# Layer border of a two-layer decoder trunk: three features made by VectorE, two more weight blocks held ahead, and the memory branch's outputs split together

## The chip, the cores and the metric

The kernel runs on one core of a Trainium2 chip. The time is the device time in microseconds of one execution; lower is better. The core has five engines that run side by side: TensorE (PE in the profile) multiplies matrices, VectorE (DVE) and ScalarE (ACT) work on tiles element by element, GpSimd (POOL) does little here, and SyncE (SP) issues the transfers from and to memory. Each engine takes its own instructions strictly in the order in which they were written, and waits on semaphores for the others.

## The reference

Two layers, each with four branches that all read the same x (512 tokens, 1024 features):

```
h = x @ w_in[l]                       # columns are shared out among the branches
y_rwkv = RWKV-7 recurrence(h...)      y_mla  = causal latent attention(h...)
y_conv = 31-tap convolution(h...)     y_mem  = attention into 256 memory tokens:
    kv = mem @ w_mem_kv;  s = q k / sqrt(128);  softmax(s) v
each branch:  y * silu(its gate columns of h)
proj   = y_n @ w_o_branch[l, n]       # per branch
merged = sum_n sigmoid(merge columns of h + b_gate) * proj
out    = merged @ w_out[l]
x      = LayerNorm(alpha * x + out) * ln_g + ln_b
```

The result of the second layer is the output.

## The kernel before

**Arithmetic.** Features lie on the partitions and tokens along the free dimension, so a projection makes 128 features by 512 tokens in PSUM. To keep fp32 accuracy with fast matmuls, every operand is split into a high half (a cast, on ScalarE as a rule) and a low half (the operand less its high half, on VectorE): `split`, line 503. Each product is then three matmuls (`mm3`, line 580). Tiles that end in h and l are such halves.

**Weights.** They are streamed. A block of 128 x 1024 numbers is loaded into one of two raw tiles (`WR = 2`, line 32), split into a high and a low tile of a pool with three pairs (`WH = 3`), and used; w123 is the 124th block, w123h and w123l its halves. `prefetch` in `stream` (line 2234) asks for the next block when fewer than `LOOK = 4` blocks are held ahead and a raw tile is free. The transfers go out on SyncE's queue (line 371).

**Order.** The kernel is written as generators: a stream of matmul items, and tasks for everything that hangs on them. At build time a planner (`Plan`, line 70) keeps a clock for each engine and a cost for each operation, and writes the instructions in the order in which its clocks let them go. So a small change of one task can move many others. Nearly all instructions go through one helper, so the profile shows line 265 for VectorE, ScalarE and GpSimd, 359 for matmuls and 364 for transposes on TensorE; groups are told apart by tile names.

**The layer border.** The second half of the output projection is the item z1 (`second_item`, line 2001; tiles pz, block 117 to 120). Its sums go through the layer norm (`out_after` and `norm`: z, lbs, lmv, lrs, lnb) and are stored to memory as xtok. To cover this, the planned `ORDER` (line 26) puts the next layer's memory work around it: keys m0 and m1 ahead of z1, keys m2 and m3 behind it (tile ps_mk, blocks 121 and 122), then m4, the memory values (`values` in `memory_items`, line 704; tile pmv, blocks 123 to 126, twelve matmuls each). Between those, `features` (line 2149) turns the normalised z back into features: four transposes into a PSUM tile xT, then xf (scale by ln_g and add ln_b), its high half xh and its low half xl; eight features, with two PSUM tiles to share. After that layer 1 begins with the latent projections (tile pl, blocks 127 on).

**The memory branch.** Four heads of attention into memory (tiles xs, xP, xt, xo) are interleaved with latent attention (scores ms, weights mP, transposes mt, output mo) and with projections and convolution taps (cacc on VectorE). Each head ends in a tile xy, which is multiplied by its gate and then split (`gate_items`, line 1830; halves yxg0 to yxg3) for the merge, which reads them much later. `turn(n)` (line 1827) says when a branch may split its outputs; for the memory branch (n = 3) it always says yes. `scaled` (line 649) gives a softmax's scaling to ScalarE or VectorE, whichever has the earlier clock in the planner.

Of the kernel before, what the change touches and what calls it, by code (L numbers as in the profile page):

```python
# [15 lines left out]
AF = mybir.ActivationFunctionType  # L16
ALU = mybir.AluOpType
# [11 lines left out]
PRI = {}  # L29
GATHER = 1500.0  # L30
RIDE = 4000.0
WR = 2
WH = 3
ALPHA = (2.0 * LAYERS) ** 0.25
# [35 lines left out]
class Plan:  # L70
# [96 lines left out]
    def run(self, stream):  # L167
# [4 lines left out]
        while True:  # L172
# [10 lines left out]
            wait = last + GATHER if self.cut == (128, 128) and not over else 0.0  # L183
            ride = RIDE if self.cut == (128, 128) and not over and last else 0.0

# [153 lines left out]
def trunk_kernel(ctx: ExitStack, tc: tile.TileContext, A, out, dbg=None):  # L339
    nc = tc.nc  # L340
    plan = Plan(tc.keep_in_program_order)
    V, S, G = Engine(plan, nc.vector, "DVE"), Engine(plan, nc.scalar, "ACT"), Engine(plan, nc.gpsimd, "POOL")
# [30 lines left out]
    def pool(bufs, **k):  # L373
        return Space(plan, ctx.enter_context(tc.tile_pool(bufs=bufs, **k)), bufs)
# [24 lines left out]
    def u(name, cols=512, dt=F32, p=128):  # L399
        return up.tile([p, cols], dt, tag="u", name=name)  # L400
# [105 lines left out]
        yield  # L506
        V.tensor_tensor(out=dst_l, in0=src, in1=dst_h.bitcast(F32), op=ALU.subtract)

    wlive = {"raw": 0, "n": 0, "hl": {}}

    x0 = []

    def weights(name, src, parts, last=False):
# [4 lines left out]
        cols = sum(parts)  # L518
        raw = wp.tile([128, 1024], F32, tag="wr", name=name, bufs=WR)[:, 0:cols]
        first = name == "w0"  # L520
# [148 lines left out]
    def close_phase():  # L669
        phase[0].close()  # L670

    def memory_items(l):

        ms = []
        res = {}

        def load(pool):
            raws = []
            for i in range(4):
                raws.append(u(f"mr{i}_{l}"))  # L680
                DMA(raws[i], A["memT"][:, 512 * i:512 * i + 512])
            hl = [[pool(f"mem{n}{i}_{l}") for n in "hl"] for i in range(4)]
            for x in "kv":
                res[x] = [[u(f"{x}m{n}{i}_{l}", 512, F32R) for n in "hl"] for i in range(2)]
            for i, (h, lo) in enumerate(hl):
                plan.due(raws[i])
                yield
                yield from split(h, lo, raws[i])
                for b in range(2):
                    c = slice(256 * b, 256 * b + 256)  # L690
                    ms.append((h[:, c], lo[:, c]))

        def keep(x, i, c, ps):
            h, lo = (y[:, c] for y in res[x][i])
            return split(h, lo, ps)

        def keys(h):
            def run(get):
                ps = yield from project(get, ms, f"mk{h}_{l}", 256)
                yield from keep("k", h // 2, slice(256 * (h % 2), 256 * (h % 2) + 256), ps)  # L700
                yield
            return run

        def values(get):
            if l:
                ps = yield from pg.take([128, 512], f"pmv{l}", 2)
            else:
                ps = [pp.tile([128, 512], F32, tag="pp", name=f"pmv0_{l}")]
                ps += yield from pa.take([128, 512], f"pmv1_{l}")
            yield from wide(get, ps, lambda k, b: [x[:, 128 * b:128 * b + 128] for x in ms[k]])  # L710

            def after():
                for i in range(2):
                    yield from keep("v", i, slice(0, 512), ps[i])
                    if l:
                        pg.free()
                if l == 0:
                    pa.free()
                MEM[l] = (res["k"], res["v"])
            plan.spawn(after())  # L720
            yield

        its = [([(A["w_mk"][l, h], (512, 512))], keys(h)) for h in range(4)]
        its += [([(A["w_mv"][l, i], (512, 512)) for i in range(4)], values)]
        return load, its, lambda: len(ms) == 8

    def layer_items(l):
        items = []
# [3 lines left out]
        def pr(n, i=0, w=1):  # L732
            return PRM[l][0][:, PCOL[n] + i:PCOL[n] + i + w]
# [749 lines left out]
        ymem = [None] * 4  # L1483
# [341 lines left out]
        added = [0] * 4  # L1825

        def turn(n):
            return n == 3 or added[{1: 3, 2: 1, 0: 2}[n]] >= 8

        def gate_items(n, base, name, ready, ys, res, op):  # L1830
            for i in range(4):
# [92 lines left out]
        def end_items():  # L1924
# [76 lines left out]
            def second_item():  # L2001

                def run(get):
                    wb = []
                    for tbs in ((0, 1), (2,), (3,)):
                        ps = yield from pg.take([128, 512], f"pz1{tbs[0]}" + t_, len(tbs))
                        for k in range(8):
                            if len(wb) <= k:
                                wb.append((yield from get()))
                            h, lo = wb[k]  # L2010
                            for o, tb in zip(ps, tbs):
                                mm3(o, *(x[:, 128 * tb:128 * tb + 128] for x in merged[k]), h, lo, k == 0, k == 7)
                            if tbs[-1] == 3:
                                free(h)
                            if k in (1, 3, 5):
                                yield

                        def after(tbs=tbs, ps=ps):
                            for o, tb in zip(ps, tbs):
                                yield from out_after(tb, o, 512)  # L2020
                                pg.free()
                        plan.spawn(after())
                        yield

                item("z1", [(A["w_out"][l, 1, i], (512, 512), i > 0 and (lambda: gates[0] == 8)) for i in range(4)], run)
# [123 lines left out]
            def features(k, zs):  # L2149
                ps, = yield from pa.take([128, 512], f"xT{k}" + t_)  # L2150
                plan.due(*zs)
                yield
                for tb in range(4):
                    TR(ps[:, 128 * tb:128 * tb + 128], zs[tb])
                yield
                f = u(f"xf{k}" + t_)
                h = xp.tile([128, 512], F32R, tag="xh", name=f"xh{k}_{l + 1}")
                lo = xp.tile([128, 512], F32R, tag="xl", name=f"xl{k}_{l + 1}")
                S.activation(f, ps, AF.Identity, scale=pr("ln_g", k), bias=pr("ln_b", k))
                pa.free()  # L2160
                turned[0] += 1
                yield from split(h, lo, f)
                while len(X[l + 1]) < k:
                    yield lambda: len(X[l + 1]) == k
                X[l + 1].append((h, lo))
                if k == 7:
                    close_phase()
                    closed[l] = True
# [46 lines left out]
    def stream(items):  # L2215


        items, todo, held, runs = list(items), [], [], []
        count, look = [0], [3]

        def pick():
            for n, (blocks, run, ready, _, _) in enumerate(items):
                if not blocks and ready is None:
                    if n == 0:
                        return n
                    break
                if ready is None or ready():
                    return n
            for n, (blocks, run, ready, _, soon) in enumerate(items):
                if soon and soon():  # L2230
                    return n
            return None

        def prefetch():
            while len(held) < look[0] + (0 if items else 2) and wlive["raw"] < WR:
                if not todo:
                    n = pick()
                    if n is None:
                        return
                    blocks, run, _, picked, _ = items.pop(n)  # L2240
                    if picked:
                        picked()
                    todo.extend(blocks)
                    runs.append(run)
                    if not blocks:
                        continue
                held.extend(weights(f"w{count[0]}", *todo.pop(0)))
                count[0] += 1

        def get():  # L2250
            while not held:
                prefetch()
                if not held:
                    yield lambda: wlive["raw"] < WR
            if not held[0]:
                yield lambda: held[0]
            w = held.pop(0)
            prefetch()
            yield plan.when(*w)
            return w  # L2260

        while items or runs:
            prefetch()
            if not runs:
                yield lambda: wlive["raw"] < WR and pick() is not None
                continue
            for cond in runs[0](get):
                prefetch()
                yield cond
            runs.pop(0)  # L2270
            look[0] = LOOK
# [106 lines left out]
```

## Time and profile before

| what | value |
|---|---|
| median of 3 runs | 1456.66 us (1456.55 to 1457.02) |
| the profiled execution, device time | 1457.49 us |
| its span, first to last instruction | 1455.5 us |
| TensorE busy | 1442.5 us (99%) |
| TensorE weight loads | 1213.7 us (83%) |
| VectorE busy | 1094.3 us (75%) |
| ScalarE busy | 690.8 us (47%) |
| TensorE's granted clock, mean | 0.999 |
| chain that ended last, share on TensorE | 94% |

The page gives one profiled execution. The timeline shows instructions with start, duration, operation and names (written tile, arrow, read tiles), and in brackets how long the engine sat idle before it and what it waited for. Matmuls overlap: the end of a matmul is modelled and lies behind the start of the next, so the distance between starts tells how fast TensorE really goes.

### The profile page before, as it was taken

How to read it: one execution, taken by the hardware profiler on the slowest of the kernel's cores; microseconds unless marked ns; L12 is line 12 of the kernel's file. 1: busy time of each engine (PE TensorE's matmuls, PEld its weight loads, DVE VectorE, ACT ScalarE, POOL GpSimd, SP SyncE). 2: the span in 40 equal slices, each digit the busy share in tenths (PEclk: the TensorE clock that was granted, in tenths of full speed). 3: DMA queues.
4: the chain of work that ended last, by engine and by line, in shares of the span. 5: the costliest groups of instructions: out<-in, count | busy, mean ns of one | idle time of the engine just before them, and what ended most of it. 6: DMA issues, size and time to landing. Idle time of an engine off the chain costs nothing.

```text
span 1455.5 us, 28372 instructions
## 1 busy us (share of the span) xinstructions
PE 1442.5 (99%) x11481; PEld 1213.7 (83%) x11481; DVE 1094.3 (75%) x2245; ACT 690.8 (47%) x1325; POOL 45.1 (3%) x79
## 2 busy tenths in 40 slices
PE   9999999999999999999999999999999999999997
PEld 9888888888888888888889878888888888888886
DVE  6799988878767786544654889988888796856756
ACT  5557754354542533443254566553263635334331
POOL 0000000000000000000000000000000000000003
PEclk9999999999999999999999999999999999999999
DMA  7454342333323233434344251622423332324422
GB/s 222 126 141 105 96 122 84 96 99 87 101 74 101 81 89 93 147 100 133 113 156 122 62 145 55 167 73 73 122 74 96 93 103 79 102 80 150 154 90 85
DMA packets 94279, 156.16 MB, mean 107 GB/s; under 512 B 44354, under 2 KB 52290, under 8 KB 94148
## 3 DMA queue, kind: packets, MB, share of 16 engines
q1 hardware_dynamic: 94148, 154.35, 36.5%
q8 instruction: 90, 1.47, 0.4%
q14 instruction: 41, 0.34, 0.1%
HBM read 135.37 MB, written 6.10 MB: 97 GB/s over the span
## 4 chain that ended last, share of the span: by engine, by line
PE 94%; DVE 3%; ACT 1%; DMA 1%; issue 0%; SPq 0%; DVEq 0%; ACTq 0%
PE ps_m L359 24%; PE po L359 12%; PE pz L359 3%; PE ps_cg L359 3%; PE ps_r L359 3%; PE ps_mg L359 3%; PE ps_val L359 3%; PE ps_rg L359 3%; PE ps_k L359 3%; PE ps_v L359 3%; PE ps_xg L359 3%; PE ps_glu L359 2%; PE ps_xq L359 2%; PE pl L359 2%; PE ms L359 2%; PE ps_mk L359 2%
## 5 line engine op out<-in xcount | busy, mean ns | idle before, releaser
L265 DVE SCALAR_TENSOR_TENSOR cacc<-hpad,prm,cacc 128x512 f32<-128x512 f32 x240 | 178.6, 746 | 3.3
L265 ACT ACTIVATE tm<-ps_m,prm 128x512 f32<-128x512 f32 x64 | 44.4, 693 | 169.4 <-PE ps_m L359 169.3
L265 DVE SCALAR_TENSOR_TENSOR mt<-tm,po 128x512 f32<-128x512 f32 x48 | 32.9, 685 | 69.3 <-PE po L359 69.1
L265 ACT ACTIVATE mP<-ms,nmm 128x128 f32<-128x128 f32 (+3 forms) x64 | 33.5, 527 | 10.1 <-DVE nmm L265 4.7
L265 DVE TENSOR_TENSOR merged<-merged,mt 128x512 f32<-128x512 f32 x48 | 33.2, 692 | 1.7
L265 DVE CUSTOM_DVE_ANT_0 ms<-ms,causal 128x128 f32<-128x128 f32 (+3 forms) x64 | 30.6, 499 | 0.3 <-PE ms L359 0.2
L265 ACT COPY mPT<-mt 128x256 f32<-128x256 f32 (+3 forms) x64 | 25.8, 429 | 8.2 <-PE mt L364 8.0
L364 PE MATMUL mt<-cst,mP 128*128 128x128 f32 x160 | 26.3, 275 | 1.6 <-DVE mP L265 1.4
L364 PEld LDWEIGHTS mt<-cst,mP 128*128 128x128 f32 x160 | 19.7, 140 | 8.9 <-DVE mP L265 1.6
L265 ACT ACTIVATE yb<-yb,mr,gr 128x64 f32<-128x64 f32 x64 | 22.1, 430 | 3.1 <-DVE mr L265 3.1
L265 DVE TENSOR_TENSOR pr<-ax,bc 128x256 f32<-128x256 f32 x64 | 22.7, 415 | 0.0
L265 POOL MEMSET D<- 128x8 f32 x8 | 0.9, 114 | 697.8 <-PE ms L359 267.6
L265 DVE SCALAR_TENSOR_TENSOR merged<-tm,po 128x512 f32<-128x512 f32 x16 | 11.0, 685 | 14.7 <-PE po L359 14.5
L265 ACT ACTIVATE Zd<-zq,cst 64x128 f32<-64x128 f32 (+1 forms) x48 | 19.2, 400 | 4.9 <-DMA zq<-scrr 4.3
L359 PE MATMUL ms<-kTl,qT 96*128 96x128 f32 (+3 forms) x64 | 21.4, 334 | 0.0
L359 PE MATMUL ms<-kTh,qTl 96*128 96x128 f32 (+3 forms) x64 | 20.6, 322 | 0.0
L359 PE MATMUL ms<-kTh,qT 96*128 96x128 f32 (+3 forms) x64 | 20.6, 321 | 0.0
L265 DVE TENSOR_REDUCE ax<-pr 128x32 f32<-128x512 f32 x32 | 20.3, 674 | 0.0
L359 PEld LDWEIGHTS mo<-mPT,v 128*64 128x64 f32 x320 | 17.3, 137 | 2.6 <-issue 2.1
L359 PE MATMUL mo<-mPT,v 128*64 128x128 f32 x320 | 19.2, 275 | 0.0
L265 ACT ACTIVATE z<-z,lnb,lrs 128x256 f32<-128x256 f32 (+1 forms) x9 | 6.1, 694 | 26.4 <-DVE lnb L265 26.4
L265 DVE SCALAR_TENSOR_TENSOR S<-w,dl,H 128x64 f32<-128x64 f32 x48 | 11.3, 278 | 9.6 <-PE w L359 9.5
(3587 smaller groups left out, 5144.7 us busy)
## 6 DMA issues: line engine op xcount, KB each, us to landing
w<-in_w_ch_dram SPq DMA_DIRECT2D x146, 512.0 KB, 3.7
w<-in_w_o_dram SPq DMA_DIRECT2D x32, 512.0 KB, 3.6
w<-in_w_out_dram SPq DMA_DIRECT2D x16, 512.0 KB, 3.5
w<-in_w_lat_dram SPq DMA_DIRECT2D x15, 336.0 KB, 3.2
w<-in_w_mk_dram SPq DMA_DIRECT2D x8, 512.0 KB, 3.5
w<-in_w_mv_dram SPq DMA_DIRECT2D x8, 512.0 KB, 3.6
w<-in_w_qk_dram SPq DMA_DIRECT2D x8, 320.0 KB, 3.0
mr<-in_memT_dram SPq DMA_DIRECT2D x8, 256.0 KB, 5.0
```

The lines of the kernel that those rows point to most:

```text
L265: return self.plan.keep(f(*a, **k))
L359: plan.keep(nc.tensor.matmul(o, lhsT, rhs, start=start, stop=stop))
L364: plan.keep(nc.tensor.transpose(o, i, ident))
```

## The change

There are three edits.

- `features`: xf is made by VectorE (a TENSOR_SCALAR with ln_g and ln_b as scalars of each partition) when the planner's clock for VectorE lies more than 300 ns behind that for ScalarE, and by ScalarE otherwise.
- `prefetch`: from the start of z1 until the memory values of the next layer are kept, two blocks more may be held ahead. The number of raw tiles and of pairs of halves is as before.
- `turn(3)`: the memory branch's outputs may be split only from when the fourth head's output is written in the program, instead of at once.

```
+AHEAD = 300.0
+MORE = 2
...
-    wlive = {"raw": 0, "n": 0, "hl": {}}
+    wlive = {"raw": 0, "n": 0, "hl": {}, "more": 0}
...
+                wlive["more"] = 0
                 MEM[l] = (res["k"], res["v"])
...
         def turn(n):
-            return n == 3 or added[{1: 3, 2: 1, 0: 2}[n]] >= 8
+            return ymem[3] is not None if n == 3 else added[{1: 3, 2: 1, 0: 2}[n]] >= 8
...
                     wb = []
+                    wlive["more"] = MORE
                     for tbs in ((0, 1), (2,), (3,)):
...
-                S.activation(f, ps, AF.Identity, scale=pr("ln_g", k), bias=pr("ln_b", k))
+                if plan.clk["DVE"] + AHEAD < plan.clk["ACT"]:
+                    V.tensor_scalar(out=f, in0=ps, scalar1=pr("ln_g", k), scalar2=pr("ln_b", k), op0=ALU.mult, op1=ALU.add)
+                else:
+                    S.activation(f, ps, AF.Identity, scale=pr("ln_g", k), bias=pr("ln_b", k))
...
-            while len(held) < look[0] + (0 if items else 2) and wlive["raw"] < WR:
+            while len(held) < look[0] + wlive["more"] + (0 if items else 2) and wlive["raw"] < WR:
```

Two lines are added near the top of the file, so what the profile of before shows as lines 265, 359 and 364 stands at 267, 361 and 366 after.

The planner turns this into other orders. On ScalarE at the border, before: the high half of block 124, five features (xf and xh, numbered 0 to 4), and then the high half of block 125.

```order
L265 CAST w124h_8141<-w124_8091 128x1024
L265 ACTIVATE xf0_0_8144<-xT0_0_8125,prm0_228 128x512
L265 CAST xh0_1_8145<-xf0_0_8144 128x512
L265 ACTIVATE xf1_0_8149<-xT1_0_8126,prm0_228 128x512
L265 CAST xh1_1_8150<-xf1_0_8149 128x512
L265 ACTIVATE xf2_0_8170<-xT2_0_8154,prm0_228 128x512
L265 CAST xh2_1_8171<-xf2_0_8170 128x512
L265 ACTIVATE xf3_0_8192<-xT3_0_8155,prm0_228 128x512
L265 CAST xh3_1_8193<-xf3_0_8192 128x512
L265 ACTIVATE xf4_0_8197<-xT4_0_8175,prm0_228 128x512
L265 CAST xh4_1_8198<-xf4_0_8197 128x512
L265 CAST w125h_8212<-w125_8163 128x1024
```

The same place after (kmh1 is the high half of the last memory key):

```order
L267 CAST w124h_8121<-w124_8068 128x1024
L267 CAST kmh1_1_7643<-ps_mk3_1_8096 128x256
L267 CAST w125h_8153<-w125_8097 128x1024
L267 ACTIVATE xf0_0_8157<-xT0_0_8131,prm0_228 128x512
L267 CAST xh0_1_8158<-xf0_0_8157 128x512
L267 ACTIVATE xf1_0_8162<-xT1_0_8132,prm0_228 128x512
L267 CAST xh1_1_8163<-xf1_0_8162 128x512
L267 CAST xh2_1_8183<-xf2_0_8182 128x512
L267 ACTIVATE xf3_0_8206<-xT3_0_8168,prm0_228 128x512
L267 CAST xh3_1_8207<-xf3_0_8206 128x512
L267 CAST w126h_8211<-w126_8169 128x1024
L267 CAST xh4_1_8215<-xf4_0_8214 128x512
```

The halves of block 125 are now made ahead of all features, those of block 126 in their midst instead of behind the fifth, and those of block 123 further up, between two layer-norm ACTIVATEs. xf2, xf4 and xf5 are gone from here. VectorE has w124l, w125l, xl0, xf2, xl1, xl2, xf4, xl3, xf5, w126l, xl4, xl5, xl6, w127l, xl7 in this order, and w123l earlier, between two of the layer norm's steps. On SyncE the transfer of block 123 now stands ahead of the six stores of xtok for the first three groups of tokens, and that of block 125 ahead of the last two.

On TensorE at the border, behind the last ps_mk matmul, before: the eight transposes of features 0 and 1, of which the last five are shown, then the first matmuls of the memory values.

```order
L364 MATMUL xT0_0_8125<-cst_81,z3_0_7156 128x128
L364 MATMUL xT1_0_8126<-cst_81,z00_0_7150 128x128
L364 MATMUL xT1_0_8126<-cst_81,z10_0_7152 128x128
L364 MATMUL xT1_0_8126<-cst_81,z20_0_7154 128x128
L364 MATMUL xT1_0_8126<-cst_81,z3_0_7156 128x128
L359 MATMUL pmv1_8129<-w123l_8113,memh0_1_7633 128x512
L359 MATMUL pmv1_8129<-w123h_8112,memh0_1_7633 128x512
```

After, at the same place, the last four of the first six value matmuls and then the first transposes:

```order
L361 MATMUL pmv1_8134<-w123h_8029,meml0_1_7634 128x512
L361 MATMUL pmv1x_8135<-w123l_8030,memh0_1_7633 128x512
L361 MATMUL pmv1x_8135<-w123h_8029,memh0_1_7633 128x512
L361 MATMUL pmv1x_8135<-w123h_8029,meml0_1_7634 128x512
L366 MATMUL xT0_0_8131<-cst_81,z00_0_7150 128x128
L366 MATMUL xT0_0_8131<-cst_81,z10_0_7152 128x128
L366 MATMUL xT0_0_8131<-cst_81,z20_0_7154 128x128
```

Six value matmuls have moved ahead of the transposes. Before, transposes came in groups of 8, 4, 8, 4, 4 and 4 with six value matmuls behind each; now six value matmuls come first, and then groups of 8, 4, 8, 8 and 4. The value matmuls of block 126 come last in both.

On VectorE in layer 1, where the first row block of latent attention meets memory attention, before: a convolution tap, a row maximum of the memory branch (nmx), the masks and row maxima of three score tiles (each pair of ISA rows), reciprocals, and the scaling of xP and of mP.

```order
L265 SCALAR_TENSOR_TENSOR cacc_1_8849<-hpad_118,prm_7650,cacc_1_8849 128x512
L265 TENSOR_REDUCE nmx_1_9416<-xs_1_9365 128x1
L265 ISA ms_1_9419,nmm_1_9432<-ms_1_9419,causal 128x128
L265 ISA nmm_1_9432 128x1
L265 ISA ms_1_9420,nmm_1_9437<-ms_1_9420,causal 128x128
L265 ISA nmm_1_9437 128x1
L265 ISA ms_1_9421,nmm_1_9442<-ms_1_9421,causal 128x256
L265 ISA nmm_1_9442 128x1
L265 RECIPROCAL smx_1_9417<-smx_1_9417 128x1
L265 RECIPROCAL smm_1_9433<-smm_1_9433 128x1
L265 TENSOR_SCALAR xP_1_9369<-xP_1_9369,smx_1_9417 128x256
L265 TENSOR_SCALAR mP_1_9431<-mP_1_9431,smm_1_9433 128x128
```

The same chain after:

```order
L267 SCALAR_TENSOR_TENSOR cacc_1_8849<-hpad_118,prm_7650,cacc_1_8849 128x512 x2
L267 ISA ms_1_9419,nmm_1_9433<-ms_1_9419,causal 128x128
L267 ISA nmm_1_9433 128x1
L267 ISA ms_1_9420,nmm_1_9438<-ms_1_9420,causal 128x128
L267 ISA nmm_1_9438 128x1
L267 ISA ms_1_9421,nmm_1_9446<-ms_1_9421,causal 128x256
L267 ISA nmm_1_9446 128x1
L267 RECIPROCAL smm_1_9434<-smm_1_9434 128x1
L267 SCALAR_TENSOR_TENSOR cacc_1_8849<-hpad_118,prm_7650,cacc_1_8849 128x512
L267 TENSOR_SCALAR mP_1_9432<-mP_1_9432,smm_1_9434 128x128
```

Two taps stand ahead of the score tiles instead of a tap and a row maximum; the scaling of xP has gone to ScalarE, and a tap stands where it was, ahead of the scaling of mP. On TensorE the four transposes of that xP (xt) now stand ahead of nine projection matmuls (ps_xq) instead of behind them, and the transposes of mP (mt) behind those nine as before. The split of yxg0 stands further back in both layers, behind the fourth head's xy; in layer 1 that of yxg3 does too, since its gate's projection has changed places with one of the latent branch. Further small swaps follow on all engines up to the middle of layer 1's recurrence.

## The prediction

> **What bounds the kernel now.** I read the page first, for which engine sets the end.
>
> ```profile
> span 1455.5 us, 28372 instructions
> ...
> PE 1442.5 (99%) x11481; PEld 1213.7 (83%) x11481; DVE 1094.3 (75%) x2245; ACT 690.8 (47%) x1325; POOL 45.1 (3%) x79
> ```
>
> TensorE is busy for all but 13.0 of 1455.5 us. No matmul is added or taken away, so the change can act only through TensorE's stops. The view of waits, for TensorE alone, names those inside the run:
>
> ```profile
> PE mt L364 <- DVE mP L265: 1.4, 2, 1.2
> PE pmv L359 <- DVE w125l L265: 1.1, 1, 1.1
> PE pl L359 <- ACT xh L265: 1.0, 1, 1.0
> PE pmv L359 <- DVE w123l L265: 0.3, 1, 0.3
> ```
>
> The change touches three of these rows. The two on pmv (memory values, layer 1) lie at the layer border, together 1.4 us; the one on mt (transposes of attention weights) lies in layer 1, where memory attention and latent attention are interleaved. The row on pl is the kernel's start, where no edit lies. The rest of the 13 us I leave out: start and tail for the most part.
>
> Next the timeline of TensorE at the border: start, duration, operation, and in brackets the idle time before it.
>
> ```profile
> 734.01 1.03 PE L364 MATMUL xT<-cst,z 128*128 128x128 f32 x8
> 735.38 0.51 PE L359 MATMUL pmv<-w123l,memh 128*128 128x512 f32 x1 [0.34 <-DVE w123l L265]
> 736.89 0.60 PE L364 MATMUL xT<-cst,z 128*128 128x128 f32 x4
> 737.25 0.48 PE L359 MATMUL pmv<-w123l,memh 128*128 128x512 f32 x1
> 738.72 1.03 PE L364 MATMUL xT<-cst,z 128*128 128x128 f32 x8
> 739.51 0.48 PE L359 MATMUL pmv<-w124l,memh 128*128 128x512 f32 x1
> 742.80 0.60 PE L364 MATMUL xT<-cst,z 128*128 128x128 f32 x4
> 744.45 0.50 PE L359 MATMUL pmv<-w125l,memh 128*128 128x512 f32 x1 [1.05 <-DVE w125l L265]
> 750.51 0.31 PE L359 MATMUL pl<-w127l,xh 128*128 128x336 f32 x1
> ```
>
> Starts tell more than brackets here. Eight transposes without a wait take 739.51 - 738.72 = 0.79 us, four take 737.25 - 736.89 = 0.36, and the six pmv matmuls after them 738.72 - 737.25 = 1.47. The first eight took 735.38 - 734.01 = 1.37, so 0.58 was lost; the four at 742.80 took 1.65, so 1.29 was lost. Together 1.87 us, against 1.39 in the brackets, because a matmul's shown duration runs on past the start of the next.
>
> Last, who is late. The windows view for that stretch (PE, PEld, DVE, ACT, POOL busy) and, above it, for a steady stretch of full matmuls:
>
> ```profile
> 680.00:690.00 10.00, 10.00 (x46) 8.28 (x45) 7.25 (x16) 4.70 (x7) 0.00 (x0) 1.00 0.49 156
> 734.01:750.51 16.50, 15.11 (x82) 12.34 (x81) 12.10 (x15) 15.57 (x24) 0.00 (x0) 1.00 0.42 136
> ```
>
> ScalarE is busy for 15.57 of 16.50 us. At the border ScalarE is the bound, though it is 47% busy overall. Its timeline there:
>
> ```profile
> 733.04 1.03 ACT L265 CAST w123h<-w 128x1024 fp32r<-128x1024 f32 x1
> 734.48 1.05 ACT L265 CAST w124h<-w 128x1024 fp32r<-128x1024 f32 x1
> 735.43 0.78 ACT L265 ACTIVATE xf<-xT,prm 128x512 f32<-128x512 f32 x1
> 736.24 0.62 ACT L265 CAST xh<-xf 128x512 fp32r<-128x512 f32 x1
> 736.77 0.77 ACT L265 ACTIVATE xf<-xT,prm 128x512 f32<-128x512 f32 x1
> 742.09 1.05 ACT L265 CAST w125h<-w 128x1024 fp32r<-128x1024 f32 x1
> 743.04 1.03 ACT L265 CAST w126h<-w 128x1024 fp32r<-128x1024 f32 x1
> ```
>
> A feature (xf, then its high half xh) costs 736.77 - 735.43 = 1.34 us, a weight's high half 743.04 - 742.09 = 0.95. Five features stand between w124h and w125h, and pmv waits for w125.
>
> **The change, part by part.** *Weights held ahead.* On SyncE's queue and on VectorE:
>
> ```profile
> 715.20 1.23 DVE L265 TENSOR_TENSOR w121l<-w,w121h 128x1024 fp32r<-128x1024 f32 x1 [1.21 <-ACT w121h L265]
> 726.15 0.54 DVE L265 TENSOR_SCALAR z<-z,lmv,lrs 128x512 f32<-128x512 f32 x1
> 734.10 1.22 DVE L265 TENSOR_TENSOR w123l<-w,w123h 128x1024 fp32r<-128x1024 f32 x1 [1.37 <-ACT w123h L265]
> 727.97 0.95 SPq L371 DMA_DIRECT2D w<-in_w_mv_dram  x2
> w<-in_w_mv_dram SPq DMA_DIRECT2D x4, 512.0 KB, 4.2
> ```
>
> Before, block 123 is asked for at 727.97, behind six stores of xtok. Now its transfer stands ahead of them. Its raw buffer is free once w121l ends (716.43), so it can land at about 716.5 + 4.2 = 720.7, and no store in the queue is held up. Its high half now stands behind the second layer-norm ACTIVATE, and its low half behind the TENSOR_SCALAR at 726.15: about 726.7 + 1.2 = 727.9. TensorE wants it at 734.01, so the 0.58 us stop has 6 us of cover. Blocks 124 and 125 move up one place: w124h takes the slot at 733.04, w125h that at 734.48, its transfer going out at about 728.4 and landing at 732.6. Their low halves follow w123l's old slot, by about 736.3 and 737.4. TensorE wants 124 after two groups of six and twelve transposes (734.01 + 2 x 1.47 + 0.79 + 0.36 = 738.1) and 125 after four groups and 28 transposes (734.01 + 4 x 1.47 + 3 x 0.79 + 0.36 = 742.6), so the 1.29 us stop goes too, with 5 us of cover. If that cover is gone, the stop comes back at its old size.
>
> *Features.* What is late next is the chain of features, because TensorE now begins with six pmv matmuls: the first four transposes start at 734.01 + 1.47 = 735.5 rather than 734.01, are done 0.4 later, and the first xf starts at about 736.0 rather than 735.43. From there ScalarE has five features at 1.34, three lone xh at 0.62, w126h at 0.95 and the smaller w127h at no more: 6.7 + 1.9 + 1.9 = 10.5 us, to 746.5. VectorE gets three TENSOR_SCALARs that read PSUM and two parameters of each row. The trace has none. Bounds: the row at 726.15, which reads SBUF (0.54), and this one, which reads PSUM with one such parameter:
>
> ```profile
> L265 DVE SCALAR_TENSOR_TENSOR ltl<-lt,prm,lth 128x512 fp32r<-128x512 f32 x10 | 7.5, 749 | 7.4 <-ACT lth L265 7.3
> ```
>
> I take 0.75, since the new ones read PSUM too. The other piece of a feature, xl, is this row:
>
> ```profile
> 736.90 0.69 DVE L265 TENSOR_TENSOR xl<-xf,xh 128x512 fp32r<-128x512 f32 x1
> ```
>
> VectorE's load from 735.3 on, where w123l ended before, is then four low halves of weights (w124 to w127, the last smaller) at no more than 1.22, eight xl at 0.69 and three xf at 0.75: 4.9 + 5.5 + 2.3 = 12.7, to 748.0, or 747.4 with the quick xf. TensorE reaches pl at 750.51 - 1.87 = 748.64, and both engines are done before that. The tightest single step I find is xf5 on VectorE. Its transposes start at 742.6 - 0.79 = 741.8 and the first four end 0.4 later, so it ends at about 743.1; TensorE wants the bank back for xT7 at 742.6 + 1.47 = 744.1. So the price of the three is nothing, hidden behind pmv; uncovered, it is at most 3 x 0.75 = 2.25.
>
> The Trainium skill, "VectorE: DVE Perf Modes", section "Why PSUM operands drop a tier", says that an fp32 operand in PSUM holds VectorE to one element a cycle, where SBUF lets a TENSOR_SCALAR take two. By that the slow end is right, and moving a PSUM read off ScalarE is worth less than the quick row suggests; by the quick row xf5 would have 0.2 us more room. No run here shows it yet.
>
> The Trainium skill, "Perfetto Trace Analysis", section "Identifying the Most-Contended Engine", says that matmul busy time is a bad measure of headroom and weight-load busy time a good one. The trace agrees with the first half: brackets would make the gain 1.39, starts make it 1.87. It does not bear out the second: in the steady stretch weight loads take 8.28 of 10 us with TensorE at full pace, so 83% leaves no 17% to win.
>
> Transposes and pmv keep their numbers; groups of transposes go from six to five, and two of 0.36 against one of 0.79 is nothing. Sum at the border: -1.87.
>
> *Gate outputs of the memory branch.* Eight splits, four a layer, keep their cost. Two move much: the one of output 0 in each layer, a cast on ScalarE and a subtraction on VectorE. The planner answers by moving matmuls around it. In layer 0 TensorE had no stop there. In layer 1 it had the one on mt:
>
> ```profile
> 862.48 0.39 PE L359 MATMUL ps_xq<-xh,w148l 128*128 128x512 f32 x1
> 864.07 0.33 PE L364 MATMUL mt<-cst,mP 128*128 128x128 f32 x1 [1.21 <-DVE mP L265]
> 861.36 0.73 DVE L265 SCALAR_TENSOR_TENSOR cacc<-hpad,prm,cacc 128x512 f32<-128x512 f32 x1
> 862.34 0.29 DVE L265 CUSTOM_DVE_ANT_0 ms<-ms,causal 128x128 f32<-128x128 f32 x1
> 863.74 0.28 DVE L265 TENSOR_SCALAR mP<-mP,smm 128x128 f32<-128x128 f32 x1
> ```
>
> From that matmul's start to mt's is 1.59 us; a full matmul holds TensorE for about 1.47 / 6 = 0.24, so 1.35 is lost. Scores, row maximum, exponent, reciprocal and scaling take 1.7 us from 862.34 on VectorE, which came to it late from convolution taps (cacc). In the new order two taps stand ahead of the same row maximum, the xP scaling leaves the chain for ScalarE, but one more tap stands before the mP scaling (0.73). So mP comes at about the same time, and four transposes of the memory branch, which stood behind mt, now stand ahead of nine projections without shortening the wait. I take 0; bounds -1.35 (stop gone) and +1.35 (a second such stop, in either layer).
>
> The outputs themselves are wanted late. These rows are the last split of layer 1 and the first matmul that reads one:
>
> ```profile
> 918.78 0.68 DVE L265 TENSOR_TENSOR yxg3l<-xy,yxg3h 128x512 fp32r<-128x512 f32 x1
> 1002.33 0.39 PE L359 MATMUL po<-yxg0l,w167h 128*128 128x512 f32 x1
> ```
>
> With 83 us between them, a split that moves by some tens of us holds nobody up.
>
> **Sum.** The profiled execution took 1457.49, 1.99 around its span. 1457.49 - 1.87 = 1455.62. It lies 0.83 above the median of 1456.66, so the median comes to 1456.66 - 1.87 = 1454.8.
>
> **Rivals.** *Both go* (0.22): the reordering also ends layer 1's stop. For it: the stop hung on VectorE being late by a tap or two. Against it: the extra tap in front of mP. -1.87 - 1.35 = -3.2, so 1453.4.
>
> *Nothing is gained* (0.14): features or lo halves come late instead and TensorE stops at pl or at a bank for xT. For it: ScalarE at 94% there, and the new xf alternating between the engines, each handing on to the other. Against it: 2.1 us of room on ScalarE, 0.6 on VectorE. 1456.7.
>
> *New stops in attention* (0.09), the slower side: in both layers the new order asks for mt after other numbers of filler matmuls, and TensorE, which takes its queue in order, stands at the mt with projections behind it. A stop costs 1.35. It turns the gain into a loss from two on: 2 x 1.35 - 1.87 = +0.83, so 1457.5. Against it: layer 0 had none of them with the same chains.
>
> **How the numbers follow.** The forecast, border alone, has 0.55: 1454.8. A measurement of this kernel can tell about 0.2% from no change, 2.9 us: below 1453.75 is faster, above 1459.6 slower. Faster needs the first rival nearly whole: 0.20. Slower needs four new stops or more: 0.03. The rest, 0.77, is no change. The range takes the first rival with a little over it, and the slower one short of its end: 1452.9 to 1457.1.
>
> **What would show it.** Right: no wait of pmv on w123l or w125l; w123l done before 730; the stretch from the last ps_mk matmul to the first pl at 14.6 us instead of 16.5; ScalarE clearly below 94% in it; three xf on VectorE at about 0.7. Wrong: a wait of pl, xT or pmv of 0.5 us or more there, or a change in layer 1's waits on mP by over 1 us either way, which would then be the larger part of the result.

## The result and the profile after

The changed kernel takes 1454.25 us (median; 1453.57 to 1455.01), the kernel before 1457.26 in the same comparison (1456.55 to 1458.16). The ratio is 0.9979, 95% interval 0.9973 to 0.9985: 3.0 us or 0.21% faster, interval 2.2 to 3.9 us. Zero lies outside the interval; by the bound of 0.2% set in the prediction the result lies on the line between no change and faster. The forecast was 1.87 us, so the time came out inside the range, but 1.1 us of gain came from somewhere that the sum had at zero. That the forecast time of 1454.8 lies only 0.55 us from the measured one is partly luck: the kernel before came out 0.60 us above the 1456.66 that the forecast started from, and this hides half of the missing gain. The profiled execution took 1454.54 us.

The page after: span, and the busy times of the engines.

```profile
span 1452.8 us, 28367 instructions
...
PE 1441.7 (99%) x11481; PEld 1214.6 (84%) x11481; DVE 1095.3 (75%) x2245; ACT 691.5 (48%) x1325; POOL 44.4 (3%) x79
```

TensorE is idle for 11.1 us instead of 13.0. The view of waits for TensorE, between 700 and 1200 us (total, times, longest):

```profile
PE xt L366 <- ACT xP L267: 0.3, 1, 0.3
PE mt L366 <- DVE mP L267: 0.3, 1, 0.3
PE mt L366 <- ACT mP L267: 0.2, 1, 0.2
```

The waits of pmv on w123l and w125l are gone, and so is the long one of mt. TensorE's timeline at the border, from the last ps_mk matmul's successor to the first pl:

```profile
733.41 0.40 PE L361 MATMUL pmv<-w123l,memh 128*128 128x512 f32 x1
734.82 1.04 PE L366 MATMUL xT<-cst,z 128*128 128x128 f32 x8
735.61 0.48 PE L361 MATMUL pmv<-w123l,memh 128*128 128x512 f32 x1
741.17 1.03 PE L366 MATMUL xT<-cst,z 128*128 128x128 f32 x8
741.96 0.48 PE L361 MATMUL pmv<-w125l,memh 128*128 128x512 f32 x1
748.00 0.32 PE L361 MATMUL pl<-w127l,xh 128*128 128x336 f32 x1
```

Eight transposes take 735.61 - 734.82 = 0.79 us here and 741.96 - 741.17 = 0.79 there, the price of eight that wait for nothing. The stretch is 748.00 - 733.41 = 14.59 us against 16.50: 1.91 less. The engines that feed it, first ScalarE:

```profile
725.07 1.04 ACT L267 CAST w123h<-w 128x1024 fp32r<-128x1024 f32 x1
733.88 1.05 ACT L267 CAST w125h<-w 128x1024 fp32r<-128x1024 f32 x1
745.97 0.62 ACT L267 CAST xh<-xf 128x512 fp32r<-128x512 f32 x1
```

And VectorE:

```profile
726.14 1.23 DVE L267 TENSOR_TENSOR w123l<-w,w123h 128x1024 fp32r<-128x1024 f32 x1
737.72 0.81 DVE L267 TENSOR_SCALAR xf<-xT,prm 128x512 f32<-128x512 f32 x1
738.45 1.47 DVE L267 TENSOR_TENSOR xl<-xf,xh 128x512 fp32r<-128x512 f32 x2
746.62 0.69 DVE L267 TENSOR_TENSOR xl<-xf,xh 128x512 fp32r<-128x512 f32 x1 [0.30 <-ACT xh L267]
```

w123l is done at 727.37, 6 us before it is wanted; w125h stands ahead of the features; the last xl ends at 747.31, 0.7 before the first pl. The windows view of the stretch (length, then PE, PEld, DVE, ACT, POOL busy):

```profile
733.41:748.00 14.59, 14.59 (x82) 12.29 (x81) 12.64 (x17) 12.69 (x20) 0.00 (x0) 1.00 0.40 128
```

ScalarE is busy for 12.69 of 14.59 us, 87%, below the 94% of before, as the prediction said.

**Where the other 1.1 us came from.** Brackets do not show it, so I compare distances between starts of the same matmuls: those that come first in a block of weights and stand ahead of and behind a region in both orders. Before:

```profile
140.63 0.39 PE L359 MATMUL pk<-ltl,w28h 128*128 128x512 f32 x1
240.40 0.40 PE L359 MATMUL ps_v<-xl,w41h 128*128 128x512 f32 x1
798.13 0.48 PE L359 MATMUL ps_val<-xl,w138h 128*128 128x512 f32 x1
905.81 0.39 PE L359 MATMUL pq<-ltl,w152h 128*128 128x512 f32 x1
963.21 0.40 PE L359 MATMUL ps_k<-xl,w160h 128*128 128x512 f32 x1
1127.58 0.39 PE L359 MATMUL ps_m<-xl,w187h 128*128 128x512 f32 x1
1190.89 0.39 PE L359 MATMUL ps_m<-xl,w196h 128*128 128x512 f32 x1
```

After:

```profile
140.21 0.39 PE L361 MATMUL pk<-ltl,w28h 128*128 128x512 f32 x1
239.81 0.40 PE L361 MATMUL ps_v<-xl,w41h 128*128 128x512 f32 x1
795.63 0.48 PE L361 MATMUL ps_val<-xl,w138h 128*128 128x512 f32 x1
903.04 0.39 PE L361 MATMUL pq<-ltl,w152h 128*128 128x512 f32 x1
960.05 0.39 PE L361 MATMUL ps_k<-xl,w160h 128*128 128x512 f32 x1
1124.42 0.39 PE L361 MATMUL ps_m<-xl,w187h 128*128 128x512 f32 x1
1187.46 0.39 PE L361 MATMUL ps_m<-xl,w196h 128*128 128x512 f32 x1
```

Layer 0's attention takes 99.60 us instead of 99.77; layer 1's, up to block 152, 107.41 instead of 107.68 and from there to block 160 57.01 instead of 57.40; a piece of layer 1's recurrence (blocks 187 to 196) 63.04 instead of 63.31. That is 0.17 + 0.27 + 0.39 + 0.27 = 1.10 us in four places, none of which the prediction had in its sum. The same rows show 0.42 us more gained ahead of block 28 (140.63 against 140.21), and behind block 196 the spans of 1455.5 and 1452.8 leave 264.61 and 265.34 us, 0.73 lost. In these two stretches TensorE's order is the same in both kernels, so I count them as spread between executions. Whether the 1.10 us are the change or chance, one execution cannot say; the experiments can.

### The profile page after: what moved, and what is told of

The parts are those of the page before. It is cut to its first block, busy times and chain, and to the rows that moved or that the text cites. A ratio compares the mean times of both kernels' runs of the same rounds, so it can differ in the third digit from the quotient of the medians.

```text
span 1452.8 us, 28367 instructions
## 1 busy us (share of the span) xinstructions
PE 1441.7 (99%) x11481; PEld 1214.6 (84%) x11481; DVE 1095.3 (75%) x2245; ACT 691.5 (48%) x1325; POOL 44.4 (3%) x79
## 4 chain that ended last, share of the span: by engine, by line
PE 98%; DVE 1%; DMA 0%; ACT 0%; SPq 0%; issue 0%; DVEq 0%
PE ps_m L361 24%; PE po L361 12%; PE pz L361 3%; PE ps_cg L361 3%; PE ps_r L361 3%; PE ps_mg L361 3%; PE ps_val L361 3%; PE ps_xg L361 3%; PE ps_rg L361 3%; PE ps_v L361 3%; PE ps_k L361 3%; PE ps_xq L361 3%; PE ps_glu L361 3%; PE ms L361 2%; PE pl L361 2%; PE ps_mk L361 2%
## 5 line engine op out<-in xcount | busy, mean ns | idle before, releaser
L267 DVE SCALAR_TENSOR_TENSOR merged<-tm,po 128x512 f32<-128x512 f32 x16 | 11.0, 686 | 14.7 <-PE po L361 14.6
```

The costliest lines, as they stand in the source:

```text
L267: return self.plan.keep(f(*a, **k))
```

## The experiments

Theory A: the border gives 1.9 us, and the edit of turn(3) gives the rest by reordering both attention regions. Theory B: the gain is the border's, and the rest is spread from one execution to the next. Times are medians; differences are against the kernel before on the same chip.

**Border alone** (turn(3) as before):

```
-            return ymem[3] is not None if n == 3 else added[{1: 3, 2: 1, 0: 2}[n]] >= 8
+            return n == 3 or added[{1: 3, 2: 1, 0: 2}[n]] >= 8
```

> The whole change without the edit of turn(3): features and blocks held ahead as in the changed kernel, both attention regions in the order of the kernel before. Theory A (the result of -3.0 us is the border, -1.9, plus stops that the reordering ended in the two attention regions, about -1.1): -1.9 us here, stretch from the last ps_mk matmul to the first pl 14.6 us, and the stop on mt of some 1.3 us in layer 1 is there as before. Theory B (the whole gain is the border; the 1.1 us outside it is spread from one execution to the next): -2.5 to -3 us here.

1454.96 against 1456.94 us, ratio 0.9987 (0.9978 to 0.9996): -2.0 us. The border's stretch is 14.6 us and the long stop on mt is back. The view of waits between 700 and 1200 us:

```profile
PE mt L366 <- DVE mP L267: 1.2, 1, 1.2
PE zw L361 <- DVE S L267: 0.4, 1, 0.4
```

This is what theory A expects. The second row, a stop in the recurrence, is in no bracket of the kernel before; it comes up again below.

**The edit of turn(3) alone:**

```
-AHEAD = 300.0
-MORE = 2
+AHEAD = 1e9
+MORE = 0
```

> Only the edit of turn(3); the border is written as in the kernel before, with its stops on w123l and w125l. Theory A: -0.7 to -1.1 us, the stop on mt of 1.35 us in layer 1 replaced by three short ones of about 0.5 each and the two later ones of 0.2 to 0.4 gone. Theory B: 0 (within 0.4 either way), whatever the trace shows of single stops.

1455.65 us, ratio 0.9990 (0.9980 to 0.9999): -1.3. The border's two stops are there, and layer 1 has the three short waits of the changed kernel. The two halves add up: -2.0 - 1.3 = -3.3, against -3.0 for both. This favours theory A, but the times alone do not settle it: the intervals are 0.6 to 3.2 us of gain for the border alone and 0.1 to 2.9 for this run. The distances in the table below do.

**The features alone** (MORE = 0, turn(3) as before):

> Only the edit of features (three of eight xf on VectorE); no more blocks held ahead, turn(3) as before. If the blocks are what ends both stops: the stop of 0.58 us on w123l stays, and the one of 1.29 on w125l shrinks only as far as the five features ahead of w125h get shorter for ScalarE (two xf of 0.72 fewer, so it is asked for 1.4 us earlier): -0.8 to -1.3 us in all. If ScalarE's load is what bounds the border: nearly the whole -1.9.

1456.03 us, ratio 0.9993 (0.9983 to 1.0002): -0.9, inside the first expectation, though zero lies in its interval. In the trace the border's stretch is 15.66 us, 0.84 less than before. The view of waits shows why it is not more:

```profile
PE pmv L361 <- DVE w123l L267: 0.3, 1, 0.3
PE pmv L361 <- DVE w125l L267: 0.2, 1, 0.2
```

The stop on w123l is whole; that on w125l is shorter, since two of the features ahead of w125h got shorter for ScalarE. The view also has the stop on mt (1.2) and one of zw on S (0.3).

**The blocks held ahead alone** (AHEAD = 1e9, turn(3) as before):

> Only the two more blocks held ahead; all eight xf on ScalarE, turn(3) as before. If the blocks alone do it: both stops on pmv gone, -1.5 to -1.9 us, though ScalarE then has 8 x 1.34 + 2 x 0.95 = 12.6 us from 736.0 on and ends at 748.6, when pl is due. If the three xf on VectorE are needed: a new stop of 0.5 us or more at pl or at a bank for xT, and -1.4 or less.

1454.86 us, ratio 0.9986 (0.9977 to 0.9995): -2.1, no less than the whole border. The windows view of the border's stretch (length, then PE, PEld, DVE, ACT, POOL busy):

```profile
733.78:748.38 14.60, 14.60 (x82) 12.24 (x81) 9.67 (x13) 13.69 (x22) 0.00 (x0) 1.00 0.42 129
```

ScalarE is busy for 13.69 of 14.60 us, 94%, the same share as before, and TensorE does not stop once. ScalarE has the same instructions as before; the stretch is shorter, and the high half of block 124 now starts ahead of it, so 1.88 us less of its work falls inside. A high share by itself does no harm: what held the border up was what stood ahead of the awaited weight halves in ScalarE's queue. Making that work lighter helped the second stop (the run above); moving the halves up ended both.

**All eight xf on VectorE** (AHEAD = -1e9, two blocks more, turn(3) as before):

> As the border alone (two more blocks, turn(3) as before), but all eight xf on VectorE instead of three. In the changed kernel VectorE was done with the border's features at 746.62 with three xf of 0.81 us; five more make 746.62 + 5 x 0.81 = 750.7, and the first pl is due at 748.0. Theory A (an xf on VectorE has a price once its cover is gone): TensorE stops for 1 to 2.7 us at an xT bank or among the first pl, and of the border's -1.9 us only 0 to -0.9 is left. Theory B (pl reads the features one after the other, 0.48 us each, so a late xl hides behind pl): no stop, -1.9 as with three.

1455.32 against 1457.11 us, ratio 0.9985 (0.9976 to 0.9994): -1.8. The same view:

```profile
733.66:748.24 14.58, 14.58 (x82) 12.29 (x81) 13.94 (x19) 7.24 (x12) 0.00 (x0) 1.00 0.38 121
```

Now VectorE is at 96%, and still no stop. Its last two xl, in VectorE's timeline:

```profile
748.39 1.46 DVE L267 TENSOR_TENSOR xl<-xf,xh 128x512 fp32r<-128x512 f32 x2
```

And the first pl of the first, the second and the eighth feature, in TensorE's:

```profile
748.24 0.32 PE L361 MATMUL pl<-w127l,xh 128*128 128x336 f32 x1
750.10 0.32 PE L361 MATMUL pl<-w127l,xh 128*128 128x336 f32 x1
761.16 0.32 PE L361 MATMUL pl<-w130l,xh 128*128 128x336 f32 x1
```

The last xl ends at 749.85, 1.6 us after the first pl. But a block of these weights serves two features, and pl takes twelve matmuls for each, three for every 128 tokens: 750.10 - 748.24 = 1.86 us. So it comes to the eighth feature only 761.16 - 748.24 = 12.9 us after its start. The 0.48 us of the expectation is the step from one group of 128 tokens to the next, not from feature to feature, so the cover was larger than theory B had it. Its outcome holds: with the blocks early, it makes no difference to TensorE which engine makes xf.

**Splits from the third head on:**

```
-            return ymem[3] is not None if n == 3 else added[{1: 3, 2: 1, 0: 2}[n]] >= 8
+            return ymem[2] is not None if n == 3 else added[{1: 3, 2: 1, 0: 2}[n]] >= 8
```

(MORE = 0, AHEAD = 1e9.)

> As the edit of turn(3) alone, but the memory branch may split its outputs from the third head on instead of the fourth. In layer 1 TensorE's order is then as with the fourth head up to the stop on mt near 862, and the splits behind it are spread out again. Theory A (the gain is at the stop on mt): the three short stops on xt and mt of about 0.33, 0.28 and 0.21 us in brackets, and the same -0.7 to -1.3 us as with the fourth head. Theory B (the gain is later, near 922, where the fourth output's gate and splits now come late): the same three short stops, but the waits near 922 as before, and half of the gain or less.

1455.77 us, ratio 0.9990 (0.9981 to 0.9999): -1.3, as with the fourth head. In the trace, layer 1 up to block 152 takes 107.33 us and the recurrence 63.03, as in the changed kernel, while the stretch between (57.19) is like the order before. So most of the edit's gain does not hang on the fourth output being late; it is there as soon as output 0 is split later. Neither theory placed it: the largest piece is in the recurrence, not at the stop on mt or near 922.

**Softmax scaling to ScalarE, by a margin of 300 ns**, on top of the changed kernel:

```
-        if plan.clk["ACT"] < plan.clk["DVE"]:
+        if plan.clk["ACT"] < plan.clk["DVE"] + 300:
```

> The changed kernel, and a softmax's scaling goes to ScalarE also where its clock in the planner is up to 300 ns behind VectorE's (20 more of them move). Theory A (the stops in the attention regions come from VectorE being late with scalings and row maxima): the waits on mP and xP of 0.82 us in brackets go, and the time is 0.5 to 1.4 us below the changed kernel's, about 1453. Theory B (which stops there are hangs on how the planner happens to mix the order, not on VectorE's load): other stops of the same size, within 0.7 us of the changed kernel either way.

1458.71 us, ratio 1.0013 (1.0004 to 1.0022): 1.6 us slower than the kernel before, 4.6 more than the changed one against its own comparison. Both expectations missed. **With a margin of 9999 ns:**

> The changed kernel with nearly all softmax scalings on ScalarE (those within 9999 ns of VectorE's clock; 57 fewer on VectorE). Theory A: as with 300 ns, 1453 or less, because ScalarE is busy for under half of the span. Theory B: no better than the changed kernel; ScalarE's queue, in which exponents and weights' high halves stand in order, makes xP and mP late in other places: 1454 to 1456.

1459.15 us, ratio 1.0015 (1.0006 to 1.0023): 2.0 slower, beyond both expectations, though theory B had the direction. The waits of this kernel between 120 and 240 us, layer 0's attention, where before and after have none:

```profile
PE mt L366 <- ACT mP L267: 1.9, 3, 1.0
PE ps_glu L361 <- ACT xql L267: 0.4, 1, 0.4
```

Layer 0 now has three waits of mt on an mP from ScalarE; in layer 1 those on mt are gone, and the one on xt is 0.7 instead of 0.3. That ScalarE is 48% busy over the whole span says nothing about how soon its queue gets to one scaling. The scaling is also longer there: one of mP, 128x512, takes 0.73 us in this run and 0.48 on VectorE in the kernel before. Which of the two weighs more was not tested. By the starts of the first matmuls of blocks 27, 42 and 98, this run is 0.1, 3.4 and 4.8 us behind the changed kernel: most is lost in layer 0's attention, and 1.4 us more up to about 610 us, in small steps that I did not trace to their causes.

**The changed kernel without the edit of features** (AHEAD = 1e9 only):

> The changed kernel with all eight xf on ScalarE again: two more blocks held ahead and the edit of turn(3) stay. Theory A (the blocks alone end both stops on pmv, and pl reads the features one by one, so moving xf earns nothing): the same as the changed kernel within 0.5 us, about -2.9 against the kernel before, the border's stretch 14.6 us. Theory B (the three xf on VectorE carry a part once the splits are moved too): 0.5 to 1 us above the changed kernel.

1453.82 against 1456.83 us, ratio 0.9976 (0.9966 to 0.9986): -3.0, the border's stretch 14.61. The edit of features earns nothing once the blocks are early.

**Layer 1's splits after latent attention:**

```
-            return ymem[3] is not None if n == 3 else added[{1: 3, 2: 1, 0: 2}[n]] >= 8
+            return ymem[3] is not None and "mla" in L if n == 3 else added[{1: 3, 2: 1, 0: 2}[n]] >= 8
```

> The changed kernel, but in layer 1 the memory branch's splits come only when latent attention is complete in the program (layer 0 and everything up to about 905 us stay in the order of the changed kernel). Theory A (splits that stand late take work out of the attention region, the later the better): 0.3 to 0.8 us below the changed kernel, waits behind 905 gone. Theory B (behind 905 no stop is left that hangs on the splits): the same as the changed kernel within 0.4.

1453.93 us, ratio 0.9977 (0.9967 to 0.9987): -2.9. Splits that come later still than with the fourth head gain nothing more.

**The changed kernel once more:**

> The changed kernel once more, on the chip of the two runs above. Theory A (border -1.9 and attention -0.7 to -1.1 in every execution, the rest varies): -2.6 to -3.0, with the bracketed waits of 0.33, 0.28 and 0.21 us on xt and mt in the same places, and other sizes only at the start, near 115 us and between 1120 and 1330 us. Theory B (the 1.1 outside the border was chance): about -1.9.

1453.84 us, ratio 0.9974 (0.9964 to 0.9985): -3.0 by the medians, and the ratio itself would be -3.8; theory B's -1.9 lies outside the interval. **And the kernel before once more:**

> The kernel before under the changed kernel's line numbers: all three edits set to do nothing, the order of every engine as before. Both theories: 1.000 within the interval, which shows how far an equal kernel comes out from 1 here; the waits on w123l (0.34 in brackets), w125l (1.05) and mP (1.21) again in the same places with the same sizes, the rest of the profile moving by up to 1 us.

1456.97 us, ratio 0.9998 (0.9989 to 1.0007). Its waits between 700 and 1200 us are those of the prediction, to 0.1 us:

```profile
PE mt L366 <- DVE mP L267: 1.2, 1, 1.2
PE pmv L361 <- DVE w125l L267: 1.1, 1, 1.1
PE pmv L361 <- DVE w123l L267: 0.3, 1, 0.3
```

Twelve traces have either the old or the new order in the attention regions and the recurrence, if the two runs on scaling are left aside. Two of them, after and the kernel before, were shown above; the distances between the same matmuls in the others are worked out in the same way:

| order of attention | kernel | w28 to w41 | w138 to w152 | w152 to w160 | w187 to w196 |
|---|---|---|---|---|---|
| old | before | 99.77 | 107.68 | 57.40 | 63.31 |
| old | before again | 99.84 | 107.65 | 57.14 | 63.52 |
| old | border alone | 99.78 | 107.65 | 57.17 | 63.98 |
| old | features alone | 99.80 | 107.68 | 57.17 | 63.79 |
| old | blocks alone | 99.80 | 107.71 | 57.36 | 63.35 |
| old | all xf on VectorE | 99.82 | 107.70 | 57.15 | 63.54 |
| new | after | 99.60 | 107.41 | 57.01 | 63.04 |
| new | changed again | 99.63 | 107.41 | 57.03 | 63.03 |
| new | no feature edit | 99.61 | 107.40 | 56.97 | 63.03 |
| new | turn(3) alone | 99.59 | 107.41 | 56.99 | 63.03 |
| new | after latent | 99.59 | 107.37 | 56.99 | 63.03 |
| third head | splits from third | 99.65 | 107.33 | 57.19 | 63.03 |

Between the two starts of a column stands the same number of full matmuls (128x512) in every trace; of the small ones a few per cent of the records are missing. So it is the order that differs. In all four columns the slowest of the new order is faster than the fastest of the old. The means differ by 0.20, 0.28, 0.23 and 0.55: 1.26 us. With the border's 1.91 that makes 3.2, and the two comparisons of the changed kernel measured 3.0. In the last column the old order varies by 0.67 us and the new by 0.01. In the old order, the spread arises between the first matmuls of blocks 189 and 190 (10.14 to 10.69 us). There stands the stop that the border alone shows:

```profile
1140.57 0.35 PE L361 MATMUL zw<-lxw,lhw 128*128 128x256 f32 x1 [0.40 <-DVE S L267]
```

zw waits for the recurrence's state S, which VectorE updates there just in time or a little late, depending on the execution. The features alone has it too, 0.30, and these two traces have the longest distances of the six. In the new order zw stands at another place among the fillers, and the wait is in none of the five traces.

## Why the prediction was right, and where it was not

- *The border, -1.87.* Right in size and mechanism: -1.91 in the trace, -2.0 by the time of the border alone. Reading the stops by starts (1.87) and not by brackets (1.39) is borne out.
- *Weights held ahead.* w123l was done at 727.37 in a trace that runs 0.59 us ahead of the one before from block 41 on (239.81 against 240.40); 727.9 was expected. Both stops went, and the blocks alone show that this edit did it by itself.
- *Features.* The price of nothing was right. "At the border ScalarE is the bound" was true of the order of before, where five features stood ahead of w125h, and the features alone, which took two xf out of that row, gave back 0.84 us; it was not true of the load, for ScalarE at 94% did no harm once the halves of blocks 123 and 125 were made earlier. The room was counted too small: I asked that all features be done at the first pl, but pl reads them one after the other and comes to the eighth 12.9 us later. So even eight xf on VectorE stayed covered, and the uncovered price, at most 2.25 us, was never tested.
- *An xf on VectorE, 0.75.* The row shows 0.81, above both bounds. What counts for the queue is the distance to the next start, 738.45 - 737.72 = 0.73.
- *Layer 1's stop on mt, "I take 0".* Nearly right: the 1.35 us came back as three short waits, with 0.28 less in all (107.68 to 107.40). TensorE's timeline after:

```profile
857.99 0.49 PE L366 MATMUL xt<-cst,xP 128*128 128x128 f32 x3
858.82 0.33 PE L366 MATMUL xt<-cst,xP 128*128 128x128 f32 x1 [0.33 <-ACT xP L267]
861.52 0.33 PE L366 MATMUL mt<-cst,mP 128*128 128x128 f32 x1 [0.28 <-DVE mP L267]
862.06 0.33 PE L366 MATMUL mt<-cst,mP 128*128 128x128 f32 x1 [0.21 <-ACT mP L267]
```

- *Gate outputs, the step that failed.* "A split that moves by some tens of us holds nobody up" is true of the outputs, but the term was put at 0 and measured -1.26 by the distances, -1.3 by the time of the edit alone. The sum saw that matmuls move with the splits, but looked for a large stop in one execution and found only the one on mt. What the reordering took away besides was small losses in layer 0 ("TensorE had no stop there"), near 922 us and in the recurrence, where the execution before happened to have the shortest distance of all six. That they are waits is inferred from the distances; only some show a bracket, like zw above and this one of the kernel before, which of the other old traces only the blocks alone has:

```profile
922.86 0.63 PE L364 MATMUL mt<-cst,mP 128*128 128x128 f32 x4 [0.21 <-DVE mP L265]
```

- *Rivals.* "Both go" had a gain of 3.2 us, the nearest to the 3.0 measured, but for a reason that did not happen: the stop on mt only broke up. "Nothing is gained" and "New stops in attention" did not come about. The latter's kind of stop is real, though: moving all the scalings made three on mt in layer 0, and that kernel was slower than before.

What stays open is why the old order's recurrence varies from 63.31 to 63.98 us from one execution to the next, and which of the moved instructions takes the 0.20 us out of layer 0.

## What to carry to other kernels

When an engine is near 100% at a stop, look first at what stands ahead of the awaited instruction in its queue: moving weight halves up took both stops away, with the same instructions on the engine. A reordered region is not free because no large stop shows there; compare distances between the same matmuls over several executions, which settled 0.2 us here where times alone had intervals of 2.6 us. And an engine's busy share over the whole span does not make it a good place for work that another engine waits for.

## What the runs showed of the hardware

An fp32 TENSOR_SCALAR of 128x512 with two parameters of each row takes 0.81 us from PSUM, where the layer norm's, with the same shape from SBUF, takes 0.54 (rows of the changed kernel). The Trainium skill, "VectorE: DVE Perf Modes", section "Why PSUM operands drop a tier", has an fp32 operand in PSUM at one element a cycle; the two rows agree with a drop. The one from SBUF, in the changed kernel:

```profile
725.55 0.54 DVE L267 TENSOR_SCALAR z<-z,lmv,lrs 128x512 f32<-128x512 f32 x1
```

Two from PSUM in a row, in the run with all xf on VectorE, take 1.52 us together, so the shown duration of one runs 0.1 us into the next:

```profile
739.70 1.52 DVE L267 TENSOR_SCALAR xf<-xT,prm 128x512 f32<-128x512 f32 x2
```
